# Channel mixers of a hybrid decoder trunk: 15 of 44 gate and value pairs from seven products of halves

## The chip, the core and the metric

The kernel runs on one core of a Trainium2 chip. The time is device time of one execution, in microseconds (us), from the first to the last instruction of the core; lower is better. The engines are called as the profile calls them: PE is TensorE (matmuls), PEld its loading of weights, DVE is VectorE, ACT is ScalarE, POOL is GpSimd, SP issues the DMAs.

## What is computed

A trunk of two layers over 256 new tokens of one sequence and 8 single tokens of running ones, all in f32: T = 264 columns, 2048 channels. Layer 0 mixes tokens by a convolution module, layer 1 by a gated linear recurrence (HGRN2). Each layer then has a channel mixer, which is where the change lies:

```python
def conv_ffn(x, buf, w_up, w_dw, b_dw, w_down):        # D_FF = 5632
    h = x @ w_up                                       # 2048 -> 2 * 5632
    h, new_buf = causal_depthwise_conv(h, buf, w_dw, b_dw)   # 3 taps
    gate, up = jnp.split(h, 2, axis=-1)
    return (jax.nn.silu(gate) * up) @ w_down, new_buf  # 5632 -> 2048

x = x + mixer(rmsnorm(x, norm_mix[i]))
x = x + conv_ffn(rmsnorm(x, norm_ffn[i]), ...)
```

## The kernel before

Channels lie on the 128 partitions and tokens along the free axis, so a matrix of activations is 16 tiles (KT) of 128x264. A tile of weights covers 128 output channels: 16 blocks of 128x128 for the first products (1 MB), 11 blocks for the second products (704 KB). The weights are what PE loads, the activations are streamed.

To keep f32 precision with one-pass matmuls, weights and activations are split into a high part, rounded to fp32r, and the remainder: w = wh + wl, h = h_high + h_low. A block then takes three matmuls, `wh*rh`, `wh*rl`, `wl*rh` (`step`, L187 to L189), each of 264 columns and each with a load of its 128x128 weights. ACT casts the high part (`split_hi`, L145), DVE subtracts for the low one (`split_lo`, L157). A few tiles elsewhere are multiplied in native f32 (L184).

All tiles stand in one list, `order`. `slot` works one off: it issues the DMA of tiles up to three ahead (`load`, on SP), emits the tile's matmuls, then what `later` has put into this turn (evacuations, conv taps, transposes), and between them the splits of tiles up to two ahead (AHEAD). The engines run exactly in the order in which the code emits for them; semaphores are set by the framework. `w`, `wh` and `wl` each have three buffers.

A channel mixer has 44 pairs, a pair being a gate tile f and a value tile 44 + f (`p_up`). Four chunks of 11 pairs run in turn; the 16 second products (`p_dn`) of a chunk follow as a block after the first products of the next chunk. A first product is multiplied by 1/rms of its column (`rstd`, L618) while it is evacuated to H, then go the three taps (L619, L624, L626), silu, gate times value, and a split of the result (`gh`, `gl`). Second products are added to x (L286). The 1/rms itself is worked out by ten DVE operations (`finish`) and one matmul of ones (`st_ffn`, L256) while the first tile's products run; three steps for the old conv state (`pre`, L605 to L607) follow.

Of the kernel before, what the change touches and what calls it, by code (L numbers as in the profile page):

```python
# [8 lines left out]
F32 = mybir.dt.float32  # L9
F32R = mybir.dt.float32r  # L10
# [7 lines left out]
P = 128  # L18
# [3 lines left out]
NB = 8  # L22
# [5 lines left out]
CHUNKS = 4  # L28
FC = FT // CHUNKS
EPS = 1e-6  # L30
# [16 lines left out]
AHEAD = 2  # L47
LOADS = 4
# [17 lines left out]
def kernel(ctx: ExitStack, tc: tile.TileContext, a: dict):  # L66
# [6 lines left out]
    wp = ctx.enter_context(tc.tile_pool(name="wp", bufs=3))  # L73
# [12 lines left out]
    cst = cp.tile([P, P + len(LV) * 64], F32, tag="cst", name="cst")  # L86
# [4 lines left out]
    ident = cst[:, :P]  # L91
# [6 lines left out]
    order = []  # L98
    for i in range(KT):
        order += [("pw1", KT + i), ("pw1", i)]  # L100
    order += [("pw2", i) for i in range(KT)]

    def ffn_order(layer):
        ups = [[(f"up{layer}", j) for f in range(c * FC, c * FC + FC) for j in (f, FT + f)] for c in range(CHUNKS)]
        dns = [[(f"dn{layer}", c * KT + n) for n in range(KT)] for c in range(CHUNKS)]
        seq = ups[0]
        for c in range(1, CHUNKS):
            seq = seq + ups[c] + dns[c - 1]
        return seq + dns[-1]

    order += ffn_order(0)
    order += HGRN
    order += [("ho", i) for i in range(KT)]
    order += ffn_order(1)

    raw, parts = {}, {}
    cnt = dict(load=0, hi=0, lo=0, use=0)

    def depth(key):
        return FC if key[0].startswith("dn") else KT  # L120

    def load(between=None):
        if cnt["load"] < len(order):
            key = order[cnt["load"]]
            w = wp.tile([P, KT, P], F32, tag="w", name=f"w_{key[0]}_{key[1]}")
            src = a[key[0]][key[1]].rearrange("p (k m) -> p k m", m=P)
            if between is None:
                nc.sync.dma_start(w[:, : depth(key), :], src)
            else:
                for k in range(0, KT, 4):  # L130
                    between(k)
                    nc.sync.dma_start(w[:, k : k + 4, :], src[:, k : k + 4, :])
            raw[key] = w
            cnt["load"] += 1

    def split_hi():
        if cnt["hi"] < len(order):
            key = order[cnt["hi"]]
            cnt["hi"] += 1
            if key in NATIVE:  # L140
                parts[key] = (raw.pop(key), None)
                return
            kk = depth(key)
            wh = wp.tile([P, KT, P], F32R, tag="wh", name=f"wh_{key[0]}_{key[1]}")
            act.copy(wh[:, :kk, :], raw[key][:, :kk, :])  # L145
            parts[key] = (wh, None)

    def split_lo():
        if cnt["lo"] < len(order):
            key = order[cnt["lo"]]  # L150
            cnt["lo"] += 1
            if key in NATIVE:
                return
            kk = depth(key)
            wl = wp.tile([P, KT, P], F32R, tag="wl", name=f"wl_{key[0]}_{key[1]}")
            wh = parts[key][0]
            vec.tensor_tensor(out=wl[:, :kk, :], in0=raw.pop(key)[:, :kk, :], in1=wh.bitcast(F32)[:, :kk, :], op=ALU.subtract)  # L157
            parts[key] = (wh, wl)

    def upto(what, fn, i):  # L160
        while cnt[what] < min(i, len(order)):
            fn()
# [18 lines left out]
    def step(pt, ww, k, last, rhs, full):  # L181
        wh, wl = ww
        if wl is None:
            pe.matmul(pt[:, :T], wh[:, k, :], full[k], start=(k == 0), stop=last)  # L184
            return
        rh, rl = rhs[k]
        pe.matmul(pt[:, :T], wh[:, k, :], rh, start=(k == 0), stop=False)  # L187
        pe.matmul(pt[:, :T], wh[:, k, :], rl, start=False, stop=False)  # L188
        pe.matmul(pt[:, :T], wl[:, k, :], rh, start=False, stop=last)  # L189

    def slot(keys, rhs, full=None, ahead=AHEAD):

        upto("hi", split_hi, cnt["use"] + len(keys))
        upto("lo", split_lo, cnt["use"] + len(keys))
        pts = []
        for key in keys:
            assert order[cnt["use"]] == key, (order[cnt["use"]], key)
            cnt["use"] += 1
            pts.append((bank(f"p_{key[0]}_{key[1]}"), parts.pop(key)))
        upto("load", load, cnt["use"] - 1 + LOADS)  # L200
        for k in range(depth(keys[0])):
            for pt, ww in pts:
                step(pt, ww, k, k == depth(keys[0]) - 1, rhs, full)
        begin, early, late = turn()
        for fn in begin:
            fn()
        upto("hi", split_hi, cnt["use"] + ahead)
        for fn in early:
            fn()
        upto("lo", split_lo, cnt["use"] + ahead)  # L210
        for fn in late:
            fn()
        return [pt for pt, _ in pts]
# [108 lines left out]
    with ExitStack() as ph:  # L322
# [179 lines left out]
        for i in range(KT):  # L502
            first = i == 0
            if i == 1:
                nc.sync.dma_start(cst, a["cst"])
                nc.sync.dma_start(a["o_conv_old"], a["cs"][:, :, 1:, :])
# [678 lines left out]
```

## Time and profile before

| | us |
|---|---|
| median of 3 runs | 2448.09 |
| lowest, highest | 2447.48, 2448.23 |
| the profiled execution | 2449.3 |
| its span, first to last instruction | 2447.5 |
| channel mixer of layer 0, by the first `p_up` and the next stage | 343 to 1121 |
| HGRN stage | 1121 to 1562 |
| channel mixer of layer 1 | 1661 to 2433 |

A row of a group reads: line, engine, operation, written tile <- read tiles, shapes, count | busy time in us, mean ns of one | idle time of the engine before them, and who ended it. Rows in order of time begin with start and length in us. PE matmuls are pipelined: one lasts longer than the distance to the next.

### The profile page before, as it was taken

Reading aid. Unit: us, or ns where it says so; the run is one execution under the profiler, and the core shown is the slowest. Engines: PE = TensorE matmul, PEld = TensorE weight load, DVE = VectorE, ACT = ScalarE, POOL = GpSimd, SP = SyncE. Lnnn points to the kernel's source line nnn. Section 1 sums busy time; section 2 is a strip of 40 time slices with the busy share of each in tenths; the row PEclk is TensorE's granted clock in tenths of the full one; section 3 lists DMA queues with packets and bytes.
Section 4 is the critical chain, followed back from the end, with each engine's and each line's share of the span. In section 5 each row is a group of like instructions: output and inputs, shape, how many; then the busy total and the mean of one; then the engine's idle time right before and its main releaser. Section 6 shows DMA issues by size and latency. Waiting matters only on the chain.

```text
span 2447.5 us, 49520 instructions
## 1 busy us (share of the span) xinstructions
PE 2413.7 (99%) x20940; PEld 2376.5 (97%) x20940; DVE 1719.4 (70%) x2908; ACT 1245.3 (51%) x2095; POOL 163.9 (7%) x234
## 2 busy tenths in 40 slices
PE   8998999999999999999999999999999999999998
PEld 7897999999999999999999999999999999999998
DVE  8998767766576567567877777757676557657655
ACT  4786645454344344345765665544444344444434
POOL 3796000000000000000000000000000000000000
PEclk9999999999999999999999999999999999999999
DMA  7453555554654554555655655555555465455453
GB/s 270 155 186 113 190 187 193 174 188 153 206 176 163 185 194 166 177 182 207 229 202 203 225 211 200 196 186 192 187 173 184 154 206 180 159 203 176 164 182 124
DMA packets 78143, 453.10 MB, mean 185 GB/s; under 512 B 8545, under 2 KB 13025, under 8 KB 39009
## 3 DMA queue, kind: packets, MB, share of 16 engines
q1 hardware_dynamic: 77920, 449.94, 53.2%
q8 instruction: 164, 2.69, 0.4%
q14 instruction: 59, 0.48, 0.1%
HBM read 436.31 MB, written 15.50 MB: 185 GB/s over the span
## 4 chain that ended last, share of the span: by engine, by line
PE 92%; DVE 5%; ACT 2%; issue 1%; DMA 0%; POOL 0%; SPq 0%; POOLq 0%; DVEq 0%; ACTq 0%
PE p_up L189 14%; PE p_up L187 14%; PE p_up L188 14%; PE p_dn L189 7%; PE p_dn L188 7%; PE p_dn L187 7%; PE p_pw L184 5%; PE p_pw L189 2%; PE p_pw L187 2%; PE p_pw L188 2%; PE p_ho L187 1%; PE p_ho L189 1%; PE p_ho L188 1%; PE p_hg L187 1%; PE p_hg L189 1%; PE p_hg L188 1%
## 5 line engine op out<-in xcount | busy, mean ns | idle before, releaser
L187 PE MATMUL p_up<-h_ffn,wh_up 128*128 128x264 f32 x2816 | 801.1, 284 | 0.7 <-DVE x L288 0.7
L189 PE MATMUL p_up<-h_ffn,wl_up 128*128 128x264 f32 x2816 | 800.7, 284 | 0.0
L188 PE MATMUL p_up<-l_ffn,wh_up 128*128 128x264 f32 x2816 | 797.5, 283 | 0.0
L145 ACT CAST wh_up<-w_up 128x2048 fp32r<-128x2048 f32 x176 | 335.9, 1909 | 506.7 <-PE p_up L188 446.8
L157 DVE TENSOR_TENSOR wl_up<-w_up,wh_up 128x2048 fp32r<-128x2048 f32 x176 | 403.6, 2293 | 231.9 <-ACT wh_up L145 231.9
L187 PEld LDWEIGHTS p_up<-h_ffn,wh_up 128*128 128x128 f32 x2816 | 530.1, 188 | 0.9 <-issue 0.9
L189 PEld LDWEIGHTS p_up<-h_ffn,wl_up 128*128 128x128 f32 x2816 | 530.1, 188 | 0.0
L188 PEld LDWEIGHTS p_up<-l_ffn,wh_up 128*128 128x128 f32 x2816 | 529.6, 188 | 0.1
L189 PE MATMUL p_dn<-gh,wl_dn 128*128 128x264 f32 x1408 | 400.8, 285 | 0.0
L187 PE MATMUL p_dn<-gh,wh_dn 128*128 128x264 f32 x1408 | 400.3, 284 | 0.0
L188 PE MATMUL p_dn<-gl,wh_dn 128*128 128x264 f32 x1408 | 400.1, 284 | 0.0
L145 ACT CAST wh_dn<-w_dn 128x1408 fp32r<-128x1408 f32 x128 | 175.9, 1374 | 325.9 <-PE p_dn L188 243.8
L157 DVE TENSOR_TENSOR wl_dn<-w_dn,wh_dn 128x1408 fp32r<-128x1408 f32 x128 | 208.1, 1626 | 108.2 <-ACT wh_dn L145 108.2
L188 PEld LDWEIGHTS p_dn<-gl,wh_dn 128*128 128x128 f32 x1408 | 265.3, 188 | 0.0
L189 PEld LDWEIGHTS p_dn<-gh,wl_dn 128*128 128x128 f32 x1408 | 264.7, 188 | 0.0
L187 PEld LDWEIGHTS p_dn<-gh,wh_dn 128*128 128x128 f32 x1408 | 264.6, 188 | 0.0
L624 DVE SCALAR_TENSOR_TENSOR C<-H,par,C 128x255 f32<-128x255 f32 x352 | 169.3, 481 | 6.3
L426 POOL TENSOR_TENSOR far<-far,z 128x230 f32<-128x230 f32 (+13 forms) x195 | 158.1, 813 | 66.2 <-ACT z L424 53.3
L286 DVE TENSOR_TENSOR x<-x,p_dn 128x264 f32<-128x264 f32 x128 | 54.9, 429 | 111.8 <-PE p_dn L189 111.8
L618 DVE TENSOR_TENSOR H<-p_up,rstd_ffn 128x264 f32<-128x264 f32 x176 | 76.1, 432 | 78.1 <-PE p_up L189 78.1
L619 ACT ACTIVATE C<-H,par 128x264 f32<-128x264 f32 x176 | 105.5, 600 | 14.0 <-DVE H L618 14.0
L184 PE MATMUL p_pw<-xg,w_pw 128*128 128x264 f32 x480 | 108.3, 386 | 0.0
(335 smaller groups left out, 4521.7 us busy)
## 6 DMA issues: line engine op xcount, KB each, us to landing
w_up<-in_up SPq DMA_DIRECT2D x176, 1024.0 KB
w_dn<-in_dn SPq DMA_DIRECT2D x128, 704.0 KB
w_pw<-in_pw SPq DMA_DIRECT2D x47, 1024.0 KB
w_hf<-in_hf SPq DMA_DIRECT2D x16, 1024.0 KB
w_hq<-in_hq SPq DMA_DIRECT2D x16, 1024.0 KB
w_hi<-in_hi SPq DMA_DIRECT2D x16, 1024.0 KB
w_hg<-in_hg SPq DMA_DIRECT2D x16, 1024.0 KB
w_ho<-in_ho SPq DMA_DIRECT2D x16, 1024.0 KB
```

What stands on the lines that cost most here:

```text
L145: act.copy(wh[:, :kk, :], raw[key][:, :kk, :])
L157: vec.tensor_tensor(out=wl[:, :kk, :], in0=raw.pop(key)[:, :kk, :], in1=wh.bitcast(F32)[:, :kk, :], op=ALU.subtract)
L184: pe.matmul(pt[:, :T], wh[:, k, :], full[k], start=(k == 0), stop=last)
L187: pe.matmul(pt[:, :T], wh[:, k, :], rh, start=(k == 0), stop=False)
L188: pe.matmul(pt[:, :T], wh[:, k, :], rl, start=False, stop=False)
L189: pe.matmul(pt[:, :T], wl[:, k, :], rh, start=False, stop=last)
L286: vec.tensor_tensor(out=x[n], in0=x[n], in1=pt[:, :T], op=ALU.add)
L426: pool.tensor_tensor(out=far, in0=far, in1=z, op=ALU.add)
L618: vec.tensor_tensor(out=h, in0=pt[:, :T], in1=rstd, op=ALU.mult)
L619: act.activation(cc, h, AF.Identity, scale=wv[:, j, 2:3], bias=pcol("ffn_b", layer * 2 * FT + j))
L624: vec.scalar_tensor_tensor(out=cc[:, d:SEQ], in0=h[:, : SEQ - d], scalar=wv[:, j, 2 - d : 3 - d], in1=cc[:, d:SEQ], op0=ALU.mult, op1=ALU.add)
```

## The change

In each mixer 15 of the 44 pairs (`PAIRED`: pairs 1, 4 and 6 of each chunk but the first) are computed by blocks of halves. The weights of the pair are seen as a 2 by 2 matrix A: row 1 the gate tile, row 2 the value tile, column 1 the first 8 blocks of depth, column 2 the last 8. The activations are B: two halves of depth by two halves of columns (H = 132). Seven products (`SEVEN`) of sums of A's quarters with sums of B's quarters give the four quarters of the result in place of eight. S1 to S4 are sums of halves of weights (`half_sum`, DVE, four of 128x1024 for each pair, made in the raw tiles); T1 to T4 are sums of quarters of the activations, made and split once for a mixer (`quarter`, `quarter_low`). Each product is 8 blocks x 3 matmuls of 132 columns into a PSUM bank; `after` adds them up to the gate and the value, seven small DVE additions of 128x132.

For this the activations must already be normalised before the products, so that the rest changes too:

- `normalised` writes xn = x * norm * rstd (16 DVE steps) during the second tile, `replaced` splits it anew into the same high and low tiles (16 ACT casts, 16 DVE subtractions) after the fourth. Only the first two pairs are still multiplied by rstd after their products (`scaled`); the others are read from PSUM by the taps.
- Chunks are 4, 8, 8, 8, 8 and 8 pairs (`DEPTHS`). The second products of a chunk are dealt out behind the pairs of the next one (`ffn_sequence`), two or four behind each pair; the last chunk's 16 stand at the end. A second product has 8 blocks (4 in the first chunk) in place of 11; there are 96 of them in place of 64, with the same number of matmuls.
- Raw weights and their split parts lie in two pools of half tiles (`Arena`): 8 raw halves in a mixer, and 8 halves for high and low parts together (6 raw halves and 12 parts in the other stages). Space is given out when the code emits; lookahead is counted in quarters of a tile (`horizon`).
- The taps, silu, gate and split go to a list (`behind`) from which `goes_on` emits as long as a count of DVE's work is not ahead of PE's (`work`), or when their result is needed (`forced`).

```diff
-CHUNKS = 4
+CHUNKS = 11
-AHEAD = 2
-LOADS = 4
+AHEAD = 8
+LOADS = 16
+RAW, RAW_FFN, PARTS, PARTS_MORE = 6, 2, 8, 4
+FFN_AHEAD = 6
+DEPTHS = (4, 8, 8, 8, 8, 8)
+PAIRED = {c + i for c in STARTS[1:] for i in (1, 4, 6)}
+SEVEN = [("A11", "B11", 0), ("S1", "T1", 1), ("S2", "T2", 2), ("S3", "T3", 3), ("A12", "B21", 0), ("S4", "B22", 1), ("A22", "T4", 3)]
...
+    def half_sum():
+        n, r = sums[cnt["sum"]]
+        A11, A12, A21, A22, S1, S2, S4 = (member(n, op) for op in ("A11", "A12", "S3", "A22", "S1", "S2", "S4"))
...
+        out, x0, x1, op = [(S1, A21, A22, ALU.add), (S2, S1, A11, ALU.subtract), (A21, A11, A21, ALU.subtract), (S4, A12, S2, ALU.subtract)][r]
...
+        vec.tensor_tensor(out=o, in0=x0, in1=x1, op=op)
...
+    def split_hi():
...
+            if len(parts.free(it)) < 2 * it.n:
+                return False
+            it.hi = parts.alloc(it.n, it)
+            it.lo = it.hi and parts.alloc(it.n, it)
...
+    def product(out, it, rhs):
+        for k in range(it.depth):
+            step(out, it, k, k == 0, k == it.depth - 1, rhs, None)
+        done(it)
...
+            def goes_on(pe_cost):
+                work["pe"] += pe_cost
+                more_loads()
+                begin, early, late = turn()
+                for fn in begin:
+                    fn()
+                more_sums(FFN_AHEAD)
+                upto("hi", split_hi, horizon(FFN_AHEAD))
+                for fn in early:
+                    fn()
+                upto("lo", split_lo, horizon(FFN_AHEAD))
+                for fn in late:
+                    fn()
+                work["dve"] = max(work["dve"], work["pe"] - 3000)
+                while back and work["dve"] < work["pe"] + 1500:
+                    cost, _, fn = back.pop(0)
+                    work["dve"] += cost
+                    fn()
...
+            def up_paired(f):
...
+                def after(n):
+                    if n == 0:
+                        act.copy(e1, ps7[0])
+                    elif n == 2:
+                        add(u2, ps7[2], e1)
+                        add(u25, ps7[1], u2)
+                    elif n == 3:
+                        add(h[1][:, H:], ps7[3], u25)
+                        add(u2, ps7[3], u2)
+                    elif n == 4:
+                        add(h[0][:, :H], ps7[4], e1)
+                    elif n == 5:
+                        add(h[0][:, H:], ps7[5], u25)
+                    elif n == 6:
+                        add(h[1][:, :H], ps7[6], u2)
+
+                for n, (op, meets, r) in enumerate(SEVEN):
+                    it = take((f"up{layer}", f, op))
...
+                    product(ps7[n], it, operand(meets))
+                    goes_on(1450)
+                    later(0, lambda n=n: after(n), first=True)
...
+            def normalised():
+                for k in range(KT):
+                    vec.scalar_tensor_tensor(out=xn[:, k, :], in0=x[k], scalar=pcol("norm_ffn", layer * KT + k), in1=rstd,
+                                             op0=ALU.mult, op1=ALU.mult)
...
+            def quarter(n):
+                name, out, x0, x1 = quarters[n]
...
+                vec.tensor_tensor(out=out, in0=x0, in1=x1, op=ALU.subtract)
+                act.copy(ts[name][0], out)
...
+            def replaced():
+                for k in range(KT):
+                    act.copy(hl[k][0], xn[:, k, :])
+                    vec.tensor_tensor(out=hl[k][1], in0=xn[:, k, :], in1=hl[k][0].bitcast(F32), op=ALU.subtract)
...
+            later(1, normalised, last=True)
+            later(2 * plain - 1, replaced, first=True)
...
+            def down(c, n):
+                end = c == len(DEPTHS) - 1
+                forced(STARTS[c] + DEPTHS[c] - 1)
+                it = take((f"dn{layer}", c, n))
+                pt = bank(f"p_dn{layer}_{c}_{n}")
+                product(pt[:, :T], it, [hidden(f) for f in range(STARTS[c], STARTS[c] + DEPTHS[c])])
+                goes_on(365 * it.depth)
```

Three places show how the order moves. The first is PE in the first mixer, at pair 5. Before, the gate tile's products begin here (`p_up_5`; h_ffn and l_ffn are the high and low parts of the activations, wh and wl those of the weights):

```order
L187 MATMUL p_up_5_4440<-h_ffn_0_2911,wh_up_5_4359 128x264
L188 MATMUL p_up_5_4440<-l_ffn_0_2920,wh_up_5_4359 128x264
L189 MATMUL p_up_5_4440<-h_ffn_0_2911,wl_up_5_4368 128x264
L187 MATMUL p_up_5_4440<-h_ffn_1_2916,wh_up_5_4359 128x264
L188 MATMUL p_up_5_4440<-l_ffn_1_2923,wh_up_5_4359 128x264
L189 MATMUL p_up_5_4440<-h_ffn_1_2916,wl_up_5_4368 128x264
```

Of the change, the end of the first of the pair's seven products and the beginning of the second (T1h and T1l are the parts of T1):

```order
L415 MATMUL p_half_5_0_4395<-h_ffn_7_3207,parts 128x132
L416 MATMUL p_half_5_0_4395<-l_ffn_7_3210,parts 128x132
L417 MATMUL p_half_5_0_4395<-h_ffn_7_3207,parts 128x132
L415 MATMUL p_half_5_1_4423<-T1h_4192,parts 128x132
L416 MATMUL p_half_5_1_4423<-T1l_4193,parts 128x132
```

The three matmuls of a block remain, with half the columns; a pair has 168 of them in place of 96.

The second place is DVE at the start of the first mixer, from the last step for the old conv state on. Before (H is an evacuated first product, C its conv, wl a split):

```order
L607 TENSOR_TENSOR pre_3766<-pre_3766,old_0_3764 128x704
L618 TENSOR_TENSOR H_0_3848<-p_up_0_3774,rstd_ffn_2796 128x264
L157 TENSOR_TENSOR wl_up_45_3906<-w_up_45_3775,wh_up_45_3901 128x2048
L624 SCALAR_TENSOR_TENSOR C_0_3849<-H_0_3848,par,C_0_3849 128x255
L624 SCALAR_TENSOR_TENSOR C_0_3849<-H_0_3848,par,C_0_3849 128x254
L626 TENSOR_TENSOR C_0_3849<-C_0_3849,pre_3766 128x8
L618 TENSOR_TENSOR H_44_3908<-p_up_44_3850,rstd_ffn_2796 128x264
L157 TENSOR_TENSOR wl_up_2_3972<-w_up_2_3851,wh_up_2_3963 128x2048
```

Of the change (`parts<-raw,parts` is a split):

```order
L864 TENSOR_TENSOR pre_3653<-pre_3653,old_0_3657 128x704
L958 TENSOR_TENSOR H_0_3784<-p_up_0_3663,rstd_ffn_2729 128x264
L362 TENSOR_TENSOR parts<-raw,parts 128x2048
L1002 SCALAR_TENSOR_TENSOR xn_3655<-x,par,rstd_ffn_2729 128x264 x16
L958 TENSOR_TENSOR H_44_3855<-p_up_44_3734,rstd_ffn_2729 128x264
L362 TENSOR_TENSOR parts<-raw_ffn_3652,parts 128x2048
L1025 TENSOR_TENSOR l_ffn_0_2847<-xn_3655,h_ffn_0_2839 128x264
```

The 16 steps of xn stand ahead of the split for the fifth tile, and 16 new low parts (the first of them is the last row here) behind it; the taps of pair 0 have moved behind those.

The third place is DVE a little later, where before the splits for tiles 4 and 48 stand:

```order
L618 TENSOR_TENSOR H_46_4172<-p_up_46_4108,rstd_ffn_2796 128x264
L157 TENSOR_TENSOR wl_up_4_4236<-w_up_4_4109,wh_up_4_4227 128x2048
L624 SCALAR_TENSOR_TENSOR C_46_4173<-H_46_4172,par,C_46_4173 128x255
L624 SCALAR_TENSOR_TENSOR C_46_4173<-H_46_4172,par,C_46_4173 128x254
L626 TENSOR_TENSOR C_46_4173<-C_46_4173,pre_3766 128x8
L640 TENSOR_TENSOR C_46_4173<-C_2_4107,C_46_4173 128x264
L618 TENSOR_TENSOR H_3_4238<-p_up_3_4176,rstd_ffn_2796 128x264
L157 TENSOR_TENSOR wl_up_48_4301<-w_up_48_4177,wh_up_48_4291 128x2048
```

Of the change (tf holds the sums of quarters; the first two rows are the splits for tiles 4 and 48):

```order
L362 TENSOR_TENSOR parts<-raw_ffn_3652,parts 128x2048
L362 TENSOR_TENSOR parts<-raw,parts 128x2048
L1014 TENSOR_TENSOR tf_3656<-xn_3655 128x1056
L1014 TENSOR_TENSOR tf_3656<-xn_3655,tf_3656 128x1056
L1019 TENSOR_TENSOR T1l_4193<-tf_3656,T1h_4192 128x1056
L1019 TENSOR_TENSOR T2l_4195<-tf_3656,T2h_4194 128x1056
L1014 TENSOR_TENSOR tf_3656<-xn_3655 128x1056
L1014 TENSOR_TENSOR tf_3656<-xn_3655,tf_3656 128x1056
L1019 TENSOR_TENSOR T3l_4197<-tf_3656,T3h_4196 128x1056
L1019 TENSOR_TENSOR T4l_4199<-tf_3656,T4h_4198 128x1056
L914 SCALAR_TENSOR_TENSOR C_2_4017<-p_up_2_3962,par,C_2_4017 128x255
L914 SCALAR_TENSOR_TENSOR C_2_4017<-p_up_2_3962,par,C_2_4017 128x254
```

The eight steps for T1 to T4 stand ahead of the taps of pairs 2 and 3, whose results the first second products (`p_dn_0_0`, PE's eleventh tile now) read.

More of the change, by code (lines that the diff above doesn't have):

```diff
@@ new lines @@
+    ffn_items(0)
+    for key in HGRN:
+        tile_item(key)
+    for i in range(KT):
+        tile_item(("ho", i))
+    ffn_items(1)
+    loads, sums = [], []
+    for n, it in enumerate(items):
+        if it.first is None:
+            loads.append((n, None))
+        elif it.first == n:
+            loads += [(n, op) for op in ("A21", "A22", "A11", "A12")]
+            sums += [(n, r) for r in range(4)]
+    cnt = dict(load=0, sum=0, hi=0, lo=0, use=0)
+    work = dict(pe=0, dve=0)
+    member = lambda first, op: items[first + [o for o, _, _ in SEVEN].index(op)]
@@ new lines, in split_lo, with upto @@
+    def split_lo():
+        if cnt["lo"] >= cnt["hi"]:
+            return False
+        it = items[cnt["lo"]]
+        if not it.native:
+            for lo, h, r in zip(parts.pieces(it.lo, it.depth, F32R), parts.pieces(it.hi, it.depth, F32), it.full()):
+                vec.tensor_tensor(out=lo, in0=r, in1=h, op=ALU.subtract)
+            raws.release(it.raw)
+            it.raw = None
+            work["dve"] += 128 * it.depth + 200
+        cnt["lo"] += 1
+        return True
+    def upto(what, fn, i):
+        while cnt[what] < min(i, len(items)):
+            if not fn():
+                return
@@ L179, in flush, with step, along @@
                     fn()
[L181 to L184, printed above, removed]
+    def step(out, it, k, first, last, rhs, full):
+        if it.native:
+            pe.matmul(out, raws.part(it.raw, k, F32), full[k], start=first, stop=last)
             return
+        wh, wl = parts.part(it.hi, k, F32R), parts.part(it.lo, k, F32R)
         rh, rl = rhs[k]
[L187 to L203, printed above, removed]
+        pe.matmul(out, wh, rh, start=first, stop=False)
+        pe.matmul(out, wh, rl, start=False, stop=False)
+        pe.matmul(out, wl, rh, start=False, stop=last)
+    def product(out, it, rhs):
+        for k in range(it.depth):
+            step(out, it, k, k == 0, k == it.depth - 1, rhs, None)
+        done(it)
+    def along(ahead=AHEAD):
         begin, early, late = turn()
@@ L665, in conv_ffn @@
+            for kind, *at in ffn_sequence():
+                if kind == "dn":
+                    down(*at)
+                    if at == [len(DEPTHS) - 1, 0]:
+                        nc.sync.dma_start(a["o_ffn_new"][layer], new)
+                elif at[0] in PAIRED:
+                    up_paired(*at)
+                else:
+                    up(*at)
             flush()
+            raws.more()
             return nxt, st
@@ L1043 @@
         hl = nxt
+    parts.more()
     _, st = conv_ffn(1, hl, st, None)
```

406 lines of the change are left out of this document (310 added, 96 removed).

## The prediction

> **What bounds the kernel now.** I read the page first: engine shares, granted clock, the chain that ended last.
>
> ```profile
> span 2447.5 us, 49520 instructions
> ...
> PE 2413.7 (99%) x20940; PEld 2376.5 (97%) x20940; DVE 1719.4 (70%) x2908; ACT 1245.3 (51%) x2095; POOL 163.9 (7%) x234
> ...
> PEclk9999999999999999999999999999999999999999
> ...
> PE 92%; DVE 5%; ACT 2%; issue 1%; DMA 0%; POOL 0%; SPq 0%; POOLq 0%; DVEq 0%; ACTq 0%
> ...
> L187 PE MATMUL p_up<-h_ffn,wh_up 128*128 128x264 f32 x2816 | 801.1, 284 | 0.7 <-DVE x L288 0.7
> ...
> L187 PE MATMUL p_dn<-gh,wh_dn 128*128 128x264 f32 x1408 | 400.3, 284 | 0.0
> ```
>
> TensorE holds 92% of the chain, at full clock. One matmul lasts 284 ns in its group, but matmuls overlap, so that is not what one costs. The cost is the distance from start to start, and the chain in order of time gives it for the second channel mixer:
>
> ```profile
> 1660.66 0.12 PE p_up L187
> ...
> 1666.52 0.45 PE st_ffn L256 x2
> ...
> 2433.14 0.87 PE p_y L1058 x8
> ```
>
> A mixer has 3 x (2816 + 1408) / 2 = 6336 such matmuls. They take 2433.14 - 1660.66 - 0.44 (the statistics matmul in between) = 772.0 us, **121.85 ns** each, with no gap. VectorE has room in these stretches (columns: length, then busy time and instructions of PE, PEld, DVE, ACT, POOL):
>
> ```profile
> 342.00:1121.00 779.00, 778.32 (x6387) 778.07 (x6386) 510.74 (x716) 351.30 (x453) 0.00 (x0) 1.00 0.53 182
> 1666.00:2433.00 767.00, 767.00 (x6296) 766.93 (x6295) 493.71 (x682) 344.39 (x444) 0.00 (x0) 1.00 0.52 176
> ```
>
> So the change is decided by two numbers: what a matmul of 132 columns costs TensorE, and whether VectorE (66% busy here) keeps up.
>
> **Term 1: TensorE's own work.** An ordinary pair is 2 tiles x 16 steps x 3 matmuls = 96 of 264 columns, 96 x 0.12185 = 11.70 us. A pair by halves is 7 products x 8 steps x 3 = 168 of 132 columns. Columns streamed fall by an eighth, but matmuls, and with them weight loads, rise by 75%: each still loads a full 128x128 tile of weights. With 30 such pairs in both mixers, 2880 matmuls (350.9 us) are replaced by 5040. No row of before has this shape (132 columns, one pass), so I bound it.
>
> From below, by streaming. Native f32 matmuls stand as two records each:
>
> ```profile
> 18.06 49.84 PE p_pw L184 x224
> ```
>
> If streaming is all that the 121.85 ns hold, half the columns take 60.9. The native records, two for a matmul, stand 49.84 / 224 = 222.5 ns apart; if each passes over its 264 columns twice, one pass is 111.3 ns, and 132 columns take 55.6. That is the lowest bound I can defend.
>
> From the side of the weights, the last statistics are the useful place. They multiply by one column (128x1, then 128x8), so almost nothing is streamed, and only loading is left:
>
> ```profile
> L1067 PE MATMUL p_ss<-ones,sq_after 128*128 128x1 f32 x4 | 0.7, 255 | 0.0
> ...
> L1067 PEld LDWEIGHTS p_ss<-ones,sq_after 128*128 128x128 f32 x4 | 0.6, 190 | 0.1
> ...
> 2434.11 0.30 PEld L1067 LDWEIGHTS p_ss<-ones,sq_after 128*128 128x128 f32 x2
> 2434.33 0.30 PEld L1067 LDWEIGHTS p_ss<-ones,acc_after 128*128 128x128 f32 x2
> 2434.55 0.30 PEld L1067 LDWEIGHTS p_ss<-ones,sq_after 128*128 128x128 f32 x2
> 2434.78 0.30 PEld L1069 LDWEIGHTS p_ss<-acc_after,ones 128*128 128x128 f32 x2
> 2435.00 0.19 PEld L1069 LDWEIGHTS p_ss<-sq_after,ones 128*128 128x128 f32 x1
> ```
>
> Eight loads in 0.89 us, **111.3 ns** from load to load, though the matmuls between them had next to nothing to do. Issue isn't the limit: 78 score matmuls with 32 columns of weights start within 0.97 us, 12 ns apart. And a load's duration grows with its columns:
>
> ```profile
> 1145.97 0.97 PE pl L812 x78
> ...
> L189 PEld LDWEIGHTS p_up<-h_ffn,wl_up 128*128 128x128 f32 x2816 | 530.1, 188 | 0.0
> ...
> L812 PEld LDWEIGHTS pl<-R 128*32 128x32 f32 x1024 | 10.8, 108 | 0.0
> ...
> L776 PEld LDWEIGHTS pv<-cst,v 128*8 128x8 f32 x16 | 1.4, 87 | 0.0
> ```
>
> (188 - 108) / 96 = 0.83 ns a column, 107 ns for 128. The mixers' one-pass weights (L189) take as long as f32 ones (190 in p_ss), so I see no faster load for them. At 264 columns such a load hides behind streaming, only just; at 132 nothing is left to hide it. So a half matmul should cost 107 to 121.85 ns (the upper end: if 121.85 is already the load's price). I take 111.3, the measured load-to-load distance. Then 5040 x 0.1113 = 561.0 us against 350.9: **+210 us**; +187 at 106.7, +263 at 121.85.
>
> The Trainium skill, "TensorE: Matmul & The Clock Gate", section "LDWEIGHTS (loading the stationary operand)", gives a load as its columns divided by 1.2, in ns, an estimate of 106.7 ns and +187 us by it. By the trace's slope that agrees; by the p_ss rows it is 5 ns short. The same page's "Back-to-back issue gap" speaks against both: rival C.
>
> **Term 2: VectorE at each mixer's start.** The order shows what is put ahead of the first second product: 16 xn (L1002), 16 new low parts (L1025), 8 steps for T1 to T4, 4 half sums, all on VectorE, which works strictly in that order, and the first chunk has only 4 pairs, so dn_0_0 waits for pair 3's gl. Prices:
>
> ```profile
> 342.97 0.37 PE L187 MATMUL p_up<-h_ffn,wh_up 128*128 128x264 f32 x1 [0.68 <-DVE x L288]
> ...
> 356.60 0.89 DVE L607 TENSOR_TENSOR pre<-pre,old 128x704 f32<-128x704 f32 x1
> 357.41 0.42 DVE L618 TENSOR_TENSOR H<-p_up,rstd_ffn 128x264 f32<-128x264 f32 x1
> ...
> L157 DVE TENSOR_TENSOR wl_up<-w_up,wh_up 128x2048 fp32r<-128x2048 f32 x176 | 403.6, 2293 | 231.9 <-ACT wh_up L145 231.9
> L157 DVE TENSOR_TENSOR wl_dn<-w_dn,wh_dn 128x1408 fp32r<-128x1408 f32 x128 | 208.1, 1626 | 108.2 <-ACT wh_dn L145 108.2
> L624 DVE SCALAR_TENSOR_TENSOR C<-H,par,C 128x255 f32<-128x255 f32 x352 | 169.3, 481 | 6.3
> L277 DVE SCALAR_TENSOR_TENSOR l_after<-x,par,h_after 128x264 fp32r<-128x264 f32 x16 | 7.8, 488 | 1.0 <-ACT h_after L268 1.0
> L618 DVE TENSOR_TENSOR H<-p_up,rstd_ffn 128x264 f32<-128x264 f32 x176 | 76.1, 432 | 78.1 <-PE p_up L189 78.1
> L145 ACT CAST wh_up<-w_up 128x2048 fp32r<-128x2048 f32 x176 | 335.9, 1909 | 506.7 <-PE p_up L188 446.8
> L626 DVE TENSOR_TENSOR C<-C,pre 128x8 f32<-128x8 f32 x88 | 14.1, 160 | 0.0
> ```
>
> The two wl rows give 1.04 ns an element: 1.23 us for 1024, 1.26 for 1056, 0.69 for 512. From 357.4 on, up to pair 3's gl: 16 xn at 0.488 (7.8), 16 low parts at 0.43 (6.9), 4 multiplications by rstd (1.7), 7 splits of a tile at 2.29 (16.0), 4 tails of a pair at 4 x 0.48 + 2 x 0.16 + 2 x 0.43 = 3.1 (12.4), 8 quarter steps (10.1), 4 half sums (4.9), 4 splits for the first second products and halves (1.4 + 2.5): 63.7 us. Pair 3's gl stands at 421.1 at the earliest. TensorE has 10 tiles before dn_0_0, 342.97 + 10 x 5.85 + 0.45 = 401.9. So it idles **at least 19 us** per mixer. In-order waits come on top: only two tiles' split parts fit in `parts` now, so a split waits for the tile two before it to be multiplied, then 1.91 us for the cast (L145) and 2.29 for the rest. Walking the order with these prices put dn_0_0 at about 435, 33 us late. I take the middle, 26 a mixer: **+52 us**, between +38 and +66. After this VectorE is no bound: a mixer sums to some 700 us (splits 371, half sums 74, small sums 31 at an assumed 0.3 each, tails 136, residuals 41, start and end 49) under TensorE's 772 + 105.
>
> **Terms at nothing.** Of the 58 ordinary pairs 54 lose their multiplications by rstd (432 ns a tile): VectorE wasn't waited for there, nothing is gained. The 210 half casts of ScalarE (1.1 us each, by L145) lie beside matmuls. Second products have the same 4224 matmuls, dealt out; their 96 residual additions in place of 64 a mixer go beside. Loads move the same bytes in smaller pieces; the DMA share is 0.53 and grows thinner with time. In the steady part a tile's split has 5.85 us (two second products) for a chain of 4.2, so 1.6 us of slack; if queues eat it, it costs up to 20 us in all, and I put in 5. The first mixer and HGRN keep lookahead and buffers: 0.
>
> **Sum.** The profiled execution took 2449.3 us (span 2447.5 and 1.8 around it), 1.2 over the median of 2448.09. 2449.3 + 210 + 52 + 5 = 2716; less that 1.2: **2715 us**. Own range: 187 + 0 + 0 gives 2635; 263 + 66 + 20 gives 2797.
>
> **Rivals.**
> B, time goes with columns (the other side, faster). If weights come in behind streaming even at 132 columns, a half matmul costs 56 to 61 ns. At 57.5: 5040 x 0.0575 = 290, 61 us saved, less 38 at the starts: about 2425. Its mechanism decides from (350.9 - 38) / 5040 = 62 ns down; above it the starts eat the gain. At 60.9 (44 saved) it is 2442, or 2456 with starts of 52. For it: nothing but the even streaming of p_pw; against it: 111.3 ns between loads with one column. Chance 0.12 (0.08 faster, 0.02 within, 0.02 slower).
>
> C, loads overlap in part. The score rows start 12 ns apart where 32 columns by the slope need 27, so loads into different column strips do overlap. If full-width loads did so by a quarter, a half matmul would cost 80 to 90: 5040 x 0.083 = 418, +67, with 52 + 5 at 2572. Against it: p_ss loads, full width, didn't. By the Trainium skill, same page, "Back-to-back issue gap", load-and-matmul pairs of 128 columns were sustained at about 81 ns, which by that estimate would be 2562; no run here shows it. Chance 0.05.
>
> D, waits for split buffers. On top of the forecast, every ordinary tile starts 1 us late (two tiles of parts in place of three): 116 tiles, +116, about 2831. For it: the slack of 1.6 us is thin; against it: half products of 2.7 us give VectorE more time than planned. Chance 0.05.
>
> **How the numbers follow.** Forecast 0.78; B 0.12; C 0.05; D 0.05. The range 2630 to 2830 is the forecast's own and the nearer half of D; it leaves out B, C and the rest of D, 0.19. Changes under 0.2% can't be told from none. Slower takes the forecast, C, D and 0.02 of B: 0.90; faster 0.08, same 0.02.
>
> **What would show it.** Right: 132-column matmuls 107 to 122 ns apart, PEld near 100% busy in a pair of halves, a pair at about 18.7 us, and TensorE idle 19 to 33 us before the first p_dn of each mixer, waiting for VectorE. Wrong: starts below 70 ns apart in a p_half product (B); VectorE or casts named as releaser in the steady part (D); no idle time before p_dn (term 2).

## The result and the profile after

| | before, beside it | after |
|---|---|---|
| median of 4 runs, us | 2448.16 | 2897.02 |
| lowest, highest, us | 2447.48, 2448.64 | 2896.48, 2899.07 |
| span of the profiled execution, us | 2447.5 | 2897.3 |

The ratio is 1.1835 (95% interval 1.1815 to 1.1856): slower by 449 us. The sign was predicted, the size was not: the forecast was +267, and 2897 lies above the range.

The page of after, its totals, the granted clock in 40 slices, and the two groups that matter:

```profile
span 2897.3 us, 56184 instructions
PE 2752.5 (95%) x23100; PEld 2704.4 (93%) x23100; DVE 2022.0 (70%) x3478; ACT 1381.2 (48%) x2429; POOL 164.4 (6%) x234
PEclk9999986799999999999999999986799999979999
L415 PE MATMUL p_dn<-g,parts 128*128 128x264 f32 x1408 | 414.1, 294 | 58.6 <-ACT g L933 46.6
L417 PE MATMUL p_half<-h_ffn,parts 128*128 128x132 f32 x720 | 212.9, 296 | 0.0
```

Two things can be read at once. TensorE was idle for 33.8 us of the span before (2447.5 - 2413.7) and is for 144.8 now (2897.3 - 2752.5): +111. And its clock, at 9 in every slice before, has three dips to 6 or 7. A matmul of 132 columns is listed at 296 ns, longer than one of 264 columns before (284), so a mean duration says nothing here; the distance between starts does. In a late, undisturbed half product it is this (in order of time: start, length):

```profile
2791.78 0.27 PE L415 MATMUL p_half<-T1h,parts 128*128 128x132 f32 x1
2791.89 0.28 PE L416 MATMUL p_half<-T1l,parts 128*128 128x132 f32 x1
2792.00 0.27 PE L417 MATMUL p_half<-T1h,parts 128*128 128x132 f32 x1
```

0.11 us, the 111 ns of Term 1. That fixes the account of TensorE's busy time. At 111.3 ns 5040 half matmuls cost 561.0 us, 210 more than the 2880 that they replace. Busy time rose by 2752.5 - 2413.7 = 338.8. The other **129 us** are TensorE at work, but more slowly than at either of its full-clock prices. So +449.8 of span is 210 + 111 + 129.

The granted clock shows most of the 129 on its own. It stands at 1 or at 0.5 in these traces, at nothing between. In after TensorE is at work for 262 us at 0.5, in before for 15; half of that is lost, 131 and 7.5, so 123 us more. What is left, some 5 us, fits the waits: the last matmul before a wait has none behind it to overlap with and counts as busy for its whole length, about 0.16 us more than its share, and TensorE has 56 waits in place of 14 (an estimate of 7 us). Laid on the matmuls, 84 of the 131 us fall on `p_half`, 28 on `p_dn` and 12 on `p_up`.

Where these half products stand: stretches of after by time. Columns: length, PE busy and matmuls, granted clock, DMA share, GB/s. First all matmuls:

```profile
443.50:482.00 38.50, 38.47 (x179) 0.50 0.25 83
522.00:556.00 34.00, 34.00 (x161) 0.50 0.27 91
2570.00:2603.00 33.00, 33.00 (x165) 0.54 0.31 102
```

The same stretches for `p_half` alone:

```profile
443.50:482.00 38.50, 34.75 (x164) 0.50 0.25 83
522.00:556.00 34.00, 31.99 (x150) 0.50 0.27 91
2570.00:2603.00 33.00, 27.26 (x128) 0.54 0.31 102
```

At 522 to 556 150 half matmuls and 11 of 264 columns take 34.0 us; at 111.3 and 121.85 ns they would take 16.7 + 1.3 = 18.0. So 16 us are lost in one pair. The other rows give 18.4 and 14.2 in the same way, and two more such stretches in the second mixer (1960 to 2003, 2045 to 2083) 17.7 and 17.2. Five stretches, with a pair by halves in each, lose 83.5 us of the 129; the other 25 pairs run at nearly their full price. How such a stretch begins (order of time; in brackets the idle time before, and who ended it):

```profile
519.70 0.30 PE L415 MATMUL p_half<-h_ffn,parts 128*128 128x132 f32 x1 [2.30 <-DVE x L519]
519.84 0.28 PE L416 MATMUL p_half<-l_ffn,parts 128*128 128x132 f32 x1
...
521.62 0.36 PE L417 MATMUL p_half<-h_ffn,parts 128*128 128x132 f32 x1
521.78 0.42 PE L415 MATMUL p_half<-h_ffn,parts 128*128 128x132 f32 x1
522.00 0.42 PE L416 MATMUL p_half<-l_ffn,parts 128*128 128x132 f32 x1
522.21 0.42 PE L417 MATMUL p_half<-h_ffn,parts 128*128 128x132 f32 x1
```

TensorE waits 2.3 us for a PSUM bank (for the bank's last reader, a residual addition of VectorE, L519), runs on at 0.11 us a matmul for 2 us, then the distance doubles to 0.21 and stays there until matmuls of 264 columns follow.

Where the 111 us of idle time are: the waits of PE in after (us in total, times, longest):

```profile
PE p_dn L415 <- ACT g L933: 46.6, 6, 9.7
PE p_dn L415 <- ACT parts L352: 12.0, 2, 6.0
PE p_up L417 <- DVE parts L362: 11.4, 13, 2.3
PE p_up L415 <- ACT parts L352: 9.8, 2, 5.0
PE p_dn L417 <- DVE parts L362: 9.5, 4, 4.1
```

And the first mixer's start and the second's, as stretches with the columns of above:

```profile
347.70:443.50 95.80, 69.03 (x491) 0.84 0.30 104
1871.10:1960.00 88.90, 66.14 (x479) 0.88 0.33 115
1960.00:2003.00 43.00, 36.85 (x171) 0.50 0.29 92
```

The starts are idle for 95.8 - 69.0 = 26.8 us, and for 22.76 + 6.15 = 28.9. The largest of these waits is that of the first second product for pair 3. It begins with pairs 0 to 2 and stops at pair 3's `g`, which ScalarE casts as soon as VectorE has worked off what stands ahead of it:

```profile
431.28 0.56 PE L415 MATMUL p_dn<-g,parts 128*128 128x264 f32 x1 [6.02 <-ACT parts L352]
442.60 0.43 DVE L932 TENSOR_TENSOR C<-C,C 128x264 f32<-128x264 f32 x1
443.07 0.41 ACT L933 CAST g<-C 128x264 fp32r<-128x264 f32 x1 [1.61 <-DVE C L932]
443.53 0.59 PE L415 MATMUL p_dn<-g,parts 128*128 128x264 f32 x1 [9.66 <-ACT g L933]
```

The rest of the two mixers is idle for another 47, mostly second products that wait for `g`, the gated activations of the chunk before (L933), and for their split weights; some 8 us lie outside the mixers.

### The profile page after: what moved, and what is told of

It is laid out like the page before. It is cut to its first block, busy times and chain, and to the rows that moved or that the text cites. A ratio compares the mean times of both kernels' runs of the same rounds, so it can differ in the third digit from the quotient of the medians.

```text
span 2897.3 us, 56184 instructions
## 1 busy us (share of the span) xinstructions
PE 2752.5 (95%) x23100; PEld 2704.4 (93%) x23100; DVE 2022.0 (70%) x3478; ACT 1381.2 (48%) x2429; POOL 164.4 (6%) x234
## 5 line engine op out<-in xcount | busy, mean ns | idle before, releaser
L362 DVE TENSOR_TENSOR parts<-raw,parts 128x1024 fp32r<-128x1024 f32 (+2 forms) x501 | 725.6, 1463 | 464.8 <-ACT parts L352 340.9
L352 ACT CAST parts<-raw 128x1024 fp32r<-128x1024 f32 (+2 forms) x501 | 612.6, 1238 | 565.3 <-PE p_half L416 165.7
L415 PE MATMUL p_up<-h_ffn,parts 128*128 128x264 f32 x1856 | 534.3, 288 | 16.0 <-ACT parts L352 9.8
L417 PE MATMUL p_up<-h_ffn,parts 128*128 128x264 f32 x1856 | 532.3, 287 | 11.4 <-DVE parts L362 11.4
L416 PE MATMUL p_up<-l_ffn,parts 128*128 128x264 f32 x1856 | 531.3, 286 | 5.4 <-DVE l_ffn L1025 5.2
L415 PE MATMUL p_dn<-g,parts 128*128 128x264 f32 x1408 | 414.1, 294 | 58.6 <-ACT g L933 46.6
L417 PE MATMUL p_dn<-g,parts 128*128 128x264 f32 x1408 | 411.9, 293 | 9.5 <-DVE parts L362 9.5
L416 PE MATMUL p_dn<-g,parts 128*128 128x264 f32 x1408 | 410.6, 292 | 0.0
L415 PEld LDWEIGHTS p_up<-h_ffn,parts 128*128 128x128 f32 x1856 | 354.1, 191 | 16.9 <-ACT parts L352 10.2
L417 PEld LDWEIGHTS p_up<-h_ffn,parts 128*128 128x128 f32 x1856 | 354.1, 191 | 14.4 <-DVE parts L362 14.4
L416 PEld LDWEIGHTS p_up<-l_ffn,parts 128*128 128x128 f32 x1856 | 353.6, 191 | 6.1 <-DVE l_ffn L1025 5.7
L415 PEld LDWEIGHTS p_dn<-g,parts 128*128 128x128 f32 x1408 | 276.4, 196 | 60.4 <-ACT g L933 48.0
L417 PEld LDWEIGHTS p_dn<-g,parts 128*128 128x128 f32 x1408 | 275.8, 196 | 10.9 <-DVE parts L362 10.8
L416 PEld LDWEIGHTS p_dn<-g,parts 128*128 128x128 f32 x1408 | 276.1, 196 | 1.1 <-DVE g L936 1.1
L415 PE MATMUL p_half<-h_ffn,parts 128*128 128x132 f32 x720 | 211.2, 293 | 6.9 <-DVE x L519 6.9
L417 PE MATMUL p_half<-h_ffn,parts 128*128 128x132 f32 x720 | 212.9, 296 | 0.0
L416 PE MATMUL p_half<-l_ffn,parts 128*128 128x132 f32 x720 | 212.5, 295 | 0.0
```

The costliest lines, as they stand in the source:

```text
L352: act.copy(h, r)
L362: vec.tensor_tensor(out=lo, in0=r, in1=h, op=ALU.subtract)
L415: pe.matmul(out, wh, rh, start=first, stop=False)
L416: pe.matmul(out, wh, rl, start=False, stop=False)
L417: pe.matmul(out, wl, rh, start=False, stop=last)
```

## The experiments

Each kernel below was timed once, with a profile; the kernel before took 2446.7 to 2449.4 us beside them, so some microseconds of difference mean nothing. The table splits every run as above: idle is span less PE's busy time, loads is 7.0 us for each pair by halves (168 x 0.1113 - 96 x 0.12185), clock is what is left of the busy time over 2413.7. "At 0.5" is the part of it that the granted clock shows: half of PE's busy time at 0.5, less before's 7.5. All of them in us:

| run | time | idle | loads | clock | at 0.5 |
|---|---|---|---|---|---|
| before | 2448 | 34 | 0 | 0 | 0 |
| after | 2897 | 145 | 210 | 129 | 123 |
| e2: 256 columns in half products | 2848 | 142 | 243 | 47 | 39 |
| e4: second products inside pairs | 2844 | 150 | 210 | 69 | 60 |
| e8: the planner's count | 2846 | 128 | 210 | 92 | 84 |
| e9: e4 + e8 + chunks moved | 2813 | 122 | 210 | 66 | 57 |
| e12: e9, no early pair | 2798 | 128 | 210 | 45 | 36 |
| e10: five pairs a mixer | 2640 | 117 | 70 | 38 | 24 |
| e11: none, e9's order | 2615 | 144 | 0 | 55 | 36 |
| e1: none, after's order | 2610 | 147 | 0 | 48 | 28 |
| e5: none, no renormalising | 2528 | 88 | 0 | 24 | 6 |
| e6: e5 with 12 parts | 2451 | 37 | 0 | -1 | -2 |

(For e2 the loads column takes 117.9 ns, measured below.) The last two columns are furthest apart, by some 20 us, where TensorE has the most waits: 101 in e1, 100 in e11, 89 in e5. There much of the clock column is overlap lost at waits, and not slow clock.

### Streams by themselves: what a matmul costs, and when the clock falls

Two kernels append streams of 240 equal one-pass matmuls to before, whose results nobody reads. In the first, "warm" streams follow on busy ones, "cold" ones a wait of about 8 us, "short" a wait of 2.3:

```diff
+    def stream(name, n, count):
+        for g in range(count // 24):
+            pt = bank(f"{name}_{g}")
+            for k in range(24):
+                pe.matmul(pt[:, :n], hl[k % KT][0][:, :P], hl[(k + 1) % KT][0][:, :n], start=k == 0, stop=k == 23)
...
+    for n in (264, 232, 200, 168, 132):
+        pause(f"wait{n}", 24)
+        stream(f"cold{n}", n, 240)
+        stream(f"then{n}", 264, 120)
```

> The kernel before with streams of one-pass matmuls added between the last mixer and the output (nothing of the result uses them): 240 matmuls each of 264, 200, 132 and 66 columns in a row, then for each of 264, 232, 200, 168 and 132 columns a wait of some 10 us, 240 matmuls of that width and 120 of 264; at the end the same for 132 after a wait of about 3 us. Theory L (a 128x128 weight load is the floor of a matmul): 122 ns from start to start at 264, and 111 at 200, at 132 and at 66 alike. Rival, columns: 122, 92, 61, 31. Theory C (after a wait the clock is at half, and a stream that leaves the array idle half of the time does not raise it): after the wait the 264 stream is back at full clock within 10 us, the 132 stream stays at 213 ns for all of its 240 matmuls (51 us) and only the 264 columns behind it raise the clock; where between 168 and 232 the border lies is open. Rival W (the clock follows the wait alone): every width is back within the same 10 us.

Groups of the run (count | busy us of the 240, mean ns of one | idle):

```profile
L1053 PE MATMUL cold<-h_ffn,h_ffn 128*128 128x132 f32 x240 | 51.7, 419 | 0.0
L1053 PE MATMUL short<-h_ffn,h_ffn 128*128 128x132 f32 x240 | 50.2, 411 | 0.0
L1053 PE MATMUL cold<-h_ffn,h_ffn 128*128 128x264 f32 x240 | 31.2, 294 | 0.0
L1053 PE MATMUL warm<-h_ffn,h_ffn 128*128 128x264 f32 x240 | 29.3, 284 | 0.0
L1053 PE MATMUL warm<-h_ffn,h_ffn 128*128 128x132 f32 x240 | 26.9, 275 | 0.0
```

The busy time over 240 is the distance: 122 ns at 264 columns, **112 at 132**, so half the columns save 8%. This is as expected, but one shape is not: 66 columns were to take 111 ns too, and lose the clock while they run (46.8 us for the 240). After a wait the two shapes part. With 264 columns the stream loses 1.9 us and is at full clock; with 132 columns it stays at 215 ns to its end, 52 us later, and a wait of 2.3 us does as much as one of 8. The second kernel varies the columns of the weights and looks for the borders of the clock ("keep": no wait, narrower and narrower):

```diff
+    for n, m_ in (264, 64), (132, 64), (132, 32), (132, 128):
+        stream(f"load{m_}w_{n}w", n, 240, m_)
...
+    for n in (192, 184, 176):
+        pause("wait", 24)
+        stream(f"cold_{n}w", n, 240)
...
+    for n in (112, 96, 80):
+        stream(f"keep_{n}w", n, 240)
```

> The kernel before with more streams of one-pass matmuls between the last mixer and the output, 240 each. Theory L says that the 111 ns come from the load of 128 columns of weights: with weights of 64 columns and 132 columns streamed they fall to 57 to 65 ns, with 32 columns of weights to no more than that, and with 128 again 111 to 112. Rival I (a fixed cost of each one-pass matmul, whatever it loads): 111 in all three. At 264 columns with 64 columns of weights L gives 110 to 113 in place of 122, if the last 10 ns come from the load beside it; 122 if they do not. From 264 to 224 columns at full weights the step from 122 to 112 lies somewhere; open where. Clock: after a wait 192 and 184 or only 192 lift it within 10 us (border between 168 and 200 so far); at full clock 112 columns are kept and 80 are not (border between 132 and 66).

```profile
L1053 PE MATMUL cold_184w<-h_ffn,h_ffn 128*128 128x184 f32 x240 | 51.7, 416 | 0.0
L1053 PE MATMUL cold_192w<-h_ffn,h_ffn 128*128 128x192 f32 x240 | 28.9, 285 | 0.0
L1053 PE MATMUL keep_96w<-h_ffn,h_ffn 128*128 128x96 f32 x240 | 45.1, 376 | 0.0
L1053 PE MATMUL keep_112w<-h_ffn,h_ffn 128*128 128x112 f32 x240 | 26.9, 275 | 0.0
L1053 PE MATMUL load64w_264w<-h_ffn,h_ffn 128*64 128x264 f32 x240 | 29.0, 282 | 0.0
L1053 PE MATMUL wide_256w<-h_ffn,h_ffn 128*128 128x256 f32 x240 | 28.3, 280 | 0.0
L1053 PE MATMUL load128w_132w<-h_ffn,h_ffn 128*128 128x132 f32 x240 | 26.9, 274 | 0.0
L1053 PE MATMUL load64w_132w<-h_ffn,h_ffn 128*64 128x132 f32 x240 | 14.8, 223 | 0.0
```

At 132 columns, weights of 64 columns in place of 128 bring the distance from 112 to 62 ns, and weights of 32 no further (14.9 us for the 240); at 264 columns they change nothing (121 against 122). So a matmul costs the larger of its load (111 for 128 columns) and its streaming (62 at 132, 121 at 264). That is Term 1 taken apart. On the clock: 192 columns for each load of 128 lift it after a wait, 184 don't; 112 keep it, 96 lose it while running. Half products lie between: they keep a full clock and cannot win one back.

### In the kernel: the same half products with more columns

Half products stream 256 columns in place of 132, with the same loads, order and waits; the values of these pairs are others than the reference's.

```diff
-                    return [tuple(t[:, k, :] for t in ts[op]) for k in range(HK)]
+                    return [tuple(t[:, min(k, HK - 2) : min(k, HK - 2) + 2, :].rearrange("p a b -> p (a b)")[:, :SEQ] for t in ts[op]) for k in range(HK)]
...
-                return [tuple(t[:, t0 : t0 + H] for t in hl[k]) for k in range(k0, k0 + HK)]
+                return [tuple(t[:, :SEQ] for t in hl[k]) for k in range(k0, k0 + HK)]
...
-                    product(ps7[n], it, operand(meets))
+                    product(banks[r][:, SEQ:] if n > 3 else banks[r][:, :SEQ], it, operand(meets))
```

> The changed kernel with each half product streaming 256 columns in place of 132 (132 of them are read afterwards; what is multiplied is no longer the right quarter, so the mixers' values differ), with the same number of matmuls and loads. Theory L: a half matmul goes from 111 to about 118 ns, 5040 x 7 = +35 us at full clock. Theory C: the array is then busy enough to get its clock back inside a pair, so most of the 130 us of slow clock goes: 2800 to 2870 us, faster than the changed kernel with twice the columns. Rival, columns: 5040 x 52 ns = +260 us, 3150. Rival W: loads as in L and the clock as in the changed kernel, about 2930.

2848.49 us: **49 us faster with nearly twice the columns**, inside what theory C gave. Its page:

```profile
span 2846.7 us, 56184 instructions
PE 2704.3 (95%) x23100; PEld 2655.0 (93%) x23100; DVE 2021.8 (71%) x3478; ACT 1382.8 (49%) x2429; POOL 164.9 (6%) x234
PEclk9999988999999999999999999998999999999999
```

TensorE is idle as long as in after (142.4 against 144.8). At 28.3 / 240 = 117.9 ns a half matmul costs 243 us over before in all, 33 more than at 111.3; yet busy time falls by 48. So 82 us of slow clock are gone (84 by the granted clock), about what the five stretches lost (83.5), and the dips are shallow. Half products lose 6 us at half clock here, in place of 84. This shows that the narrow stream, and not the waits alone, held the clock down there. The 47 us that stay, 39 of them at half clock, are what these waits cost with wide streams too.

### Parts of the change without half products

e1 empties the set of pairs and keeps all else; e5 also leaves out xn, the new low parts and T1 to T4, and multiplies every pair by 1/rms after its products, as before; e6 gives e5 the pool of 12 halves of parts that the other stages have.

```diff
-PAIRED = {c + i for c in STARTS[1:] for i in (1, 4, 6)}
+PAIRED = set()
...
-                    if f < plain:
+                    if True:
...
-            later(1, normalised, last=True)
-            later(2 * plain - 1, replaced, first=True)
...
-            later(2 * plain, quarters_made, last=True)
...
-RAW, RAW_FFN, PARTS, PARTS_MORE = 6, 2, 8, 4
+RAW, RAW_FFN, PARTS, PARTS_MORE = 6, 2, 12, 0
```

> The changed kernel with no pair by halves (PAIRED empty); xn, the new high and low parts and T1 to T4 are still made at each start, and the second products are dealt out. Theory L+C: the 210 us of loads go, and the half clock lasts only shortly after each wait; what is left is the waits at the two starts and a little clock, 2500 to 2580 us. Rival W or buffers (the waits and the smaller buffers are the cost, not the half products): 2650 or more.

> No pair by halves, and no xn, new parts or T1 to T4: all products are multiplied by rstd after their matmuls as before; the pools of halves, the chunks of 4 and 8 pairs and the second products dealt out stay. If the starts' VectorE work is what made the no-halves kernel 163 us slower: 2470 to 2510. If it is the smaller pool of split parts: 2540 or more, with p_up waiting for splits.

> The one before this with 12 halves for split parts in the mixers in place of 8 (room that xn and T1 to T4 leave). If the pool of parts makes p_up wait for its splits: these waits go, 2450 to 2470. If not: within 5 us of the run with 8.

2610.03, 2527.79 and 2451.43. e1 missed what was expected: without a single half product 163 us are lost, not 50 to 130. The steps down say to what. The new chunks, the dealing out and the other pools cost 4 us (e6, which came as expected). The pool of 8 halves costs 76 (e6 to e5), and renormalising at the starts 82 (e5 to e1). e5 fell between its two expectations, nearer to the pool. PE's largest wait in e5:

```profile
PE p_up L417 <- DVE parts L362: 45.4, 68, 2.3
```

And in e1:

```profile
PE p_up L417 <- DVE parts L362: 36.8, 59, 2.3
```

With 8 halves a third ordinary tile finds no room, its split begins only when an earlier tile is done, and TensorE waits 0.7 us at 68 tiles: rival D, in kernels without half products. In after that row is down to 11.4. A likely reason, not tested by itself, is that a half product asks for two halves of parts at a time in place of four and gives VectorE longer. So these two terms of e1 must not be added to after as they stand.

### Waits taken out of after

e4 lets two second products run inside each pair by halves (`INSIDE = (2, 4)`, behind its third and fifth product), so that `g` and banks get time and a wide stream comes sooner. e8 corrects a count: `goes_on` is told 1450 ns for a half product, which takes 24 x 0.111 = 2.67 us, so the taps and gates in its list come late.

```diff
-                    goes_on(1450)
+                    goes_on(2670)
```

> The changed kernel with the two second products behind a pair by halves moved into it (one after the third product, one after the fifth); the work is the same. Theory C: a pair that begins at half clock is back at full clock with the first second product (264 columns) inside it; five such pairs of some 37 us in the changed kernel lose 19 us each, of which 10 come back: 2830 to 2870 us. Rival W: the clock does not depend on what runs, 2890 to 2905.

> The changed kernel with one number of the planner altered: a half product counts 2670 ns of PE work in place of 1450 (24 x 111 ns as measured). If the 7 us waits for gh at the ends of chunks come from tails put off because the planner thinks PE has done little: these waits (4 of them, 27 us in all) and the half clock behind them go, 2840 to 2870. If tails are late because VectorE is full: 2885 or more.

2844.16 and 2845.58, both as expected. The wait for `g` in e8, against 46.6 in after:

```profile
PE p_dn L415 <- ACT g L933: 32.8, 4, 9.7
```

Idle time falls by 16, the clock term by 37: here each microsecond of idle time takes more than two of slow clock with it, since it stood before half products (they lose 56 us at half clock, 84 in after). In e4 idle time doesn't fall at all (150) and the clock term by 60: half products lose 23 us at half clock. e9 puts both together, with the short chunk last but one and the first pairs by halves at 4 and 6:

```diff
-DEPTHS = (4, 8, 8, 8, 8, 8)
+DEPTHS = (8, 8, 8, 8, 4, 8)
...
-PAIRED = {c + i for c in STARTS[1:] for i in (1, 4, 6)}
+PAIRED = {4, 6, 33} | {c + i for c in (8, 16, 24, 36) for i in (1, 4, 6)}
...
-        plain = DEPTHS[0] // 2
+        plain = 2
```

> The changed kernel with three things altered that leave its work the same: two second products stand inside each pair by halves, a half product counts 2670 ns in the planner, and the chunks are 8, 8, 8, 8, 4, 8 pairs, so that the first second product comes four pairs later; still 15 pairs by halves a mixer. If the 450 us are 210 of loads, 111 of waits and 129 of slow clock, the last two mostly go and the loads stay: 2670 to 2730. If the half products bring waits of their own that no order avoids: 2780 or more. If loads were not the floor: under 2600.

2813.47, a miss: 210 of loads stand as they must, but idle time is still 122 and the clock term 66. It lies in the range expected if half products bring waits of their own. Is it tied to the pairs? e10 has five pairs a mixer in e9's order, e11 none.

```diff
-PAIRED = {4, 6, 33} | {c + i for c in (8, 16, 24, 36) for i in (1, 4, 6)}
+PAIRED = {12, 20, 28, 33, 40}
...
-PAIRED = {12, 20, 28, 33, 40}
+PAIRED = set()
```

> The one before this with 5 pairs by halves a mixer in place of 15, the other 10 ordinary. Theory L: 7.0 us a pair (168 x 111.3 - 96 x 121.85 ns), 20 pairs fewer: 140 us under the run with 15, less what ordinary tiles wait for the smaller pool of parts (0.7 us for a pair or so, 14 us).

> The same again with no pair by halves; xn, the new parts and T1 to T4 are still made. Theory L: another 70 us under the run with five, less the same waits; 2510 to 2550, of which some 75 are the pool of 8 halves and the rest the starts.

2640.47 and 2614.92. e10 came out lower than expected: 173 us under e9, not some 126 to 140. From e10 to e9 20 pairs cost 173 us: 140 of loads, 29 of clock, 4 of idle time. From e11 to e10 ten pairs cost only 26, since idle time falls by 27 and the clock term by 17, against 70 of loads; the splits that tiles wait for go from 56.5 to 29.5 us. So e11, like e1, missed. It has as much idle time and slow clock without a half product as e9 with 30 pairs, but not the same waits: 56.5 us of its idle time are waits of ordinary tiles for splits, against 14.8 in e9, where 19 us stand before half products. How much of e9's idle time half products bring is not separated by these runs.

Last, e9's two stretches at half clock, with pairs 4 and 6 at the starts. Columns: length, PE busy and matmuls, granted clock, DMA share, GB/s:

```profile
420.00:460.00 40.00, 38.21 (x197) 0.56 0.17 58
1920.00:1960.00 40.00, 38.20 (x202) 0.58 0.17 54
```

e12 moves these two pairs to 23 and 31:

```diff
-PAIRED = {4, 6, 33} | {c + i for c in (8, 16, 24, 36) for i in (1, 4, 6)}
+PAIRED = {23, 31, 33} | {c + i for c in (8, 16, 24, 36) for i in (1, 4, 6)}
```

> As e9_waits_out, but no pair by halves stands in the first eight: two pairs, 4 and 6, go to 23 and 31; the count of 15 a mixer stays. In e9 the only long stretches at half clock were these pairs, right behind the waits at the start of each mixer (granted clock 0.56 at 420 to 460 us and 0.58 at 1920 to 1960). If the slow clock comes from a wait followed by matmuls of 132 columns: these stretches go, 2 x 17 to 2 x 20 us, and TensorE's idle time stays near e9's 122 us: 2770 to 2785, busy time of TensorE near 2650. If the slow clock comes from the waits alone, whatever stands behind them: 2805 to 2820. If pairs behind one another (22 and 23, 30 and 31) bring waits of their own: more than 2820.

```profile
420.00:460.00 40.00, 30.75 (x228) 0.87 0.30 106
460.00:500.00 40.00, 31.65 (x239) 0.87 0.38 125
```

(PE's part and the clock of the first row are the same in e11, which has no pairs.) 2798.26, between two of the expectations. The half-clock stretches are gone, and with them 22 us of busy time, not 34 to 40: ordinary tiles stand in the same waits now and lose clock too (0.87), and idle time is 6 us longer. By the granted clock half products lose 33 us at 0.5 in e9 and nothing in e12, all other matmuls 32 and 43. So the 36 us of e12 over before, like the 39 of e2 and the 28 of e1, are what waits cost where streams of 256 or 264 columns follow. e12 is the fastest kernel with all 30 pairs, and 349 us behind before; no kernel of this study is faster than before.

## Why the prediction was right or wrong

**Term 1, +210: right.** It said 111.3 ns for a half matmul, from eight loads in a statistics stage; after shows 0.11 us, the streams 112. The trace of before could carry it because weights of 128 columns cost the same behind 1, 132 and 200 columns (111 to 112 ns). Rival C (80 to 90 ns) is out, and rival B's 61 ns are what is left once loads are shortened (62 at weights of 64 columns): the price of the streaming was right too, only it isn't the larger of the two.

**Term 2, +52 at the starts: right in size.** 26.8 and 28.9 us idle against 19 to 33 foretold for each mixer, and the wait foretold is there: pair 3's `g`, behind VectorE's queue. It comes later than foretold, though. The first second product begins at 431.3 us in the first mixer, against "about 435", but without pair 3; that part follows at 443.5. TensorE also came there later, by a start of the mixer at 347.7 in place of 343.0 and by slow clock, so the idle time agrees in part by luck. Between e5 and e1, with the small pool and without pairs, renormalising costs more (59 of idle time and 22 at half clock): the start costs more than its idle time.

**"In the steady part ... I put in 5": wrong, 47.** The 1.6 us of slack were counted for ordinary tiles, and half products were taken to give VectorE more time. At chunk ends that did not help: the planner's 1450 ns hold work back that TensorE then waits for. e8 shows 16 us of it. The rest are waits for split weights and for `g` at chunk ends, which e4's and e9's orders move about and don't remove; which instruction of VectorE is at fault for each was not tried.

**The step that failed: the sum priced TensorE's clock at nothing.** No term stood for it: the prediction read the clock as full in every slice of before, gave each matmul its full-clock price and added the idle time as idle time alone. The runs show 129 us in its place. 82 to 84 come from half products that follow a wait, run at 213 ns and cannot lift the clock: five stretches lose 83.5, and with 256 columns 82 to 84 are gone (e2). Some 40 are what waits take from the matmuls of 264 columns behind them, as in e2 (39) and e12 (36), and some 5 the overlap of matmuls that each wait ends. With 129 for the clock and 47 for the steady waits in place of 0 and 5, the sum gives 2715 + 129 + 42 = 2886; 8 us of idle time outside the mixers, priced at 0, and 4 more at the starts make it 2898, against 2897 measured.

**Rival D** (2831, waits for split buffers) names a real wait: 76 us in e5 against e6. In after it is small, 11.4 us before ordinary tiles. The time came out nearest to D for another reason.

## What to carry to other kernels

Fewer columns for each load of weights is no saving once the load is the longer part: count matmuls by the larger of load and streaming. At the sizes here, with 128 columns of weights and 132 streamed, an algorithm that trades an eighth of the streamed columns for 75% more loads loses before its additions are paid. Price a new wait of TensorE twice, once as idle time and once as the clock that follows, and ask whether the stream behind it is wide enough to get the clock back. A stage where TensorE never waits hides this; its trace shows a full clock and no sign of how near the border is.

## What the runs showed of the hardware that was not expected

- A wait of 2.3 us can be enough to halve the granted clock, and the fall can come some 2 us after work has begun again (519.7 and 521.8 us in after; a 2.3 us wait did the same in the streams). In after the clock stays at 0.5 for multiples of about 3.4 us: 3.4, 6.8, 10.2, 34.1, 37.5 and 58.0.
- Whether the clock comes back depends on the columns streamed for each load: with weights of 128 columns, 192 lift it and 184 don't in 52 us; 112 keep it and 96 lose it. Why the two borders differ is open; one run each.
- At half clock the load of weights takes twice as long too: matmuls of 132 columns go from 112 to 215 ns, though their streaming alone would need about 2 x 62 = 124 (an estimate). The Trainium skill, "TensorE: Matmul & The Clock Gate", section "What's actually happening", says that what is issued in the first 3.4 us or so runs at the low clock and everything after at full clock. The streams of 264 columns agree (1.9 us lost after a wait, which is 3.8 us of work at half clock); those of 184 and fewer don't, and for them the measurement decides: TensorE was busy without a gap for 51.7 us and stayed slow.
